# Rolling the columns of a matrix in HBM: DMA engines 516 rows apart in place of 4

## The chip, the cores and the metric

The kernel runs on one core of a Trainium2 chip. The metric is the device time of one execution in microseconds (us), the median of several runs. The work is nearly all DMA: 16 DMA engines of the core copy from HBM to HBM. Instructions on SP (SyncE), ACT (ScalarE) and POOL (GpSimd) issue the DMAs, each in its own queue; the 16 engines take the work of all queues.

## The reference

```
x = randn(8192, 8192) as float32, shift = 100
return np.roll(x, shift, axis=1)
```

Each row of 8192 numbers (32 KiB) is turned to the right by 100 places: columns 100 to 8191 of the output are columns 0 to 8091 of the input, and the last 100 columns of the input come first. Nothing is computed, and rows don't depend on each other.

## The kernel before

The output's columns are cut at `a` = 128, the shift rounded up to a multiple of 128; `g` = 28 is the rest. The columns from 128 on are the **main copy**: 8064 numbers, 32,256 bytes in each row, copied straight from `x` to `out`, both in HBM (L33 to L36). The first 128 columns, the **heads**, go through on-chip memory (L55 to L75): POOL loads small pieces into the tiles `t` and `h` (L66, L67, L70), VectorE puts the pieces together (L68, L71), and POOL stores them (L75). The heads are 8.39 MB of the DMA queues' 272.70 MB, and run beside the main copy in the first third of the time.

The main copy is one DMA for 16 rows. The 16 rows of a DMA are given to the 16 DMA engines, one to each. In the view `(c e j) w -> c j e w`, with 16 values of `e` and 4 of `j`, engine `e` gets row 64c + 4e + j: the engines stand 4 rows (128 KiB) apart within one block of 64 rows (2 MiB). The loop over `j` is the inner one, so that an engine takes four neighbouring rows one after the other; then `c` goes to the next block. DMAs with even `j` are issued by SP, with odd `j` by ACT: 256 each. No order between the DMAs is needed; each queue's issue waits for the DMA that it issued four places earlier, so that up to four DMAs of a queue are in flight.

The 18 DMAs of the heads are issued by POOL and wait only for each other and for VectorE's copies.

Of the kernel before, what the change touches and what calls it, by code (L numbers as in the profile page):

```python
# [1 line left out]

# [4 lines left out]


@with_exitstack
def kernel(  # L10
    ctx: ExitStack,
    tc: tile.TileContext,
    x: bass.AP,
    shift: int,
    out: bass.AP,
):
    nc = tc.nc
    n_rows, n_cols = x.shape
    s = shift % n_cols
    a = -(-s // 128) * 128  # L20
    g = a - s
    P = nc.NUM_PARTITIONS
    engines = [nc.sync, nc.scalar]
    n_chunks = 16
    rows = n_rows // n_chunks

    xm = x.rearrange("(c e j) w -> c j e w", e=16, j=4)
    om = out.rearrange("(c e j) w -> c j e w", e=16, j=4)
    if a < n_cols:  # L33
        for c in range(n_rows // 64):
            for j in range(4):
                engines[j % 2].dma_start(out=om[c, j, :, a:], in_=xm[c, j, :, g:n_cols - s])  # L36
    if a == 0:
        return


    if a > 512:
        for i in range(n_chunks):
            r = slice(i * rows, (i + 1) * rows)
            nc.gpsimd.dma_start(out=out[r, :s], in_=x[r, n_cols - s:])
            if g > 0:
                nc.gpsimd.dma_start(out=out[r, s:a], in_=x[r, :g])
        return

    Q, J = 4, 8
    n_st = n_rows // (P * Q * J)
    reads = ctx.enter_context(tc.tile_pool(name="reads", bufs=n_st))  # L55
    heads = ctx.enter_context(tc.tile_pool(name="heads", bufs=n_st))
    xt = x.rearrange("(k p j q) c -> k q p j c", q=Q, j=J, p=P)
    ot = out.rearrange("(k p j q) c -> k q p j c", q=Q, j=J, p=P)
    tiles = []
    for k in range(n_st):  # L60
        t = reads.tile([P, Q - 1, J, a], x.dtype)
        h = heads.tile([P, Q, J, a], x.dtype)
        for q in range(1, Q):
            lead = bass.AP(tensor=x.tensor, offset=(k * P * J * Q + q) * n_cols - s,
                           ap=[[J * Q * n_cols, P], [Q * n_cols, J], [1, a]])
            nc.gpsimd.dma_start(out=t[:, q - 1], in_=lead)  # L66
        nc.gpsimd.dma_start(out=h[:, Q - 1, :, :s], in_=xt[k, Q - 1, :, :, n_cols - s:])  # L67
        nc.vector.tensor_copy(h[:, :Q - 1, :, :s], t[:, :, :, :s])  # L68
        if g > 0:
            nc.gpsimd.dma_start(out=h[:, 0, :, s:], in_=xt[k, 0, :, :, :g])  # L70
            nc.vector.tensor_copy(h[:, 1:, :, s:], t[:, :, :, s:])  # L71
        tiles.append(h)
    for k, h in enumerate(tiles):
        for q in range(Q):
            nc.gpsimd.dma_start(out=ot[k, q, :, :, :a], in_=h[:, q])  # L75


# [1 line left out]
_INS = ['x', 'shift']  # L79
_OUTS = [((8192, 8192), 'float32')]  # L80

_NUMBERS = {'shift': 100}


# [26 lines left out]
```

## Time and profile before

| what | value |
|---|---|
| median of 7 runs | 821.04 us (818.74 to 822.83) |
| the profiled execution | 820.11 us, of which the span is 818.3 |
| instructions | 589; VectorE busy 3.7 us, POOL 16.1 us |
| issue of a main DMA on SP, on ACT | 0.51 us, 0.52 us (median) |
| main DMA from issue to landing | 12.5 us (median) |
| all DMAs that write `out`, from issue to landing | 4.1 us (least), 115.9 us (most) |

The span is the time from the first to the last instruction of the profiled execution. The page cuts it into 40 equal slices and gives, for each, the busy share of the DMA engines in tenths and the GB/s that they moved, counting each byte once. In the list of DMA queues, q1 is the queue of SP, q10 that of ACT and q0 that of POOL: the columns are packets, megabytes (MB), and the time that the packets took as a share of 16 engines over the stretch shown. A row of the main copy is one packet of 32,256 bytes and one of 4 bytes that reports its completion.

A line of waits gives who waited, at which line, for what: the sum in us, how often, and the longest. In the table of stretches, a line begins with the stretch, its length, the busy time of VectorE and POOL, and ends with the granted clock, the busy share of the DMA engines and the GB/s moved.

### The profile page before, as it was taken

To read this page: it belongs to the slowest core of one execution; us is meant where nothing else is said; L and a number is where in the kernel's file an instruction comes from. 1 tells how busy PE (TensorE), PEld (TensorE's weight loads), DVE (VectorE), ACT (ScalarE), POOL (GpSimd) and SP (SyncE) were. 2 spreads that over 40 slices of the span, in tenths; PEclk is the share of its full clock that TensorE was granted. 3 is DMA by queue.
4 is the path that set the end of the run, shared out by engine and by line. 5 is a ranking of instruction groups with operands and counts; after the bars stand their busy time and mean duration, and the time that the engine had idled before them with its cause. 6 is when DMAs were issued, how large, how long until landed. Compare 5 with 4: busy or idle time off the path is not lost. (4 is left out here: it accounts for less than half of the span.)

```text
span 818.3 us, 589 instructions
## 1 busy us (share of the span) xinstructions
DVE 3.7 (0%) x4; POOL 16.1 (2%) x22
## 2 busy tenths in 40 slices
DVE  0000000000000000000000000000000000000000
POOL 3001001000000000000000000000000000000000
DMA  9999999999999999999999999999999999999997
GB/s 301 335 341 334 330 344 361 356 351 351 342 352 335 326 328 334 341 326 336 334 330 328 339 328 334 337 331 331 334 326 337 337 325 333 330 333 337 328 337 255
DMA packets 18724, 272.70 MB, mean 333 GB/s; under 512 B 8480, under 2 KB 8480, under 8 KB 10528
## 3 DMA queue, kind: packets, MB, share of 16 engines
q1 hardware_dynamic: 8192, 132.14, 48.2%
q10 hardware_dynamic: 8192, 132.14, 46.3%
q0 software_dynamic: 2336, 8.39, 4.4%
q14 instruction: 4, 0.03, 0.0%
HBM read 268.44 MB, written 268.44 MB: 656 GB/s over the span
## 5 line engine op out<-in xcount | busy, mean ns | idle before, releaser
L75 POOL DMA_DIRECT2D out_dram<-h x8 | 6.9, 957 | 90.5 <-DMA h<-in_x_dram 79.5
L66 POOL DMA_DIRECT2D t<-in_x_dram x6 | 5.4, 912 | 0.8 <-PEq L106 0.8
L68 DVE COPY h<-t 128x2400 f32<-128x2400 f32 x2 | 2.8, 1410 | 115.8 <-DMA t<-in_x_dram 115.8
L67 POOL DMA_DIRECT2D h<-in_x_dram x2 | 1.8, 884 | 17.5 <-DMA t<-in_x_dram 17.5
L70 POOL DMA_DIRECT2D h<-in_x_dram x2 | 1.8, 884 | 13.1 <-DMA t<-in_x_dram 13.1
L71 DVE COPY h<-t 128x672 f32<-128x672 f32 x2 | 1.0, 505 | 0.0
L92 POOL MEMSET const-float32-0.0<- 128x1 f32 x1 | 0.1, 100 | 0.2 <-issue 0.2
L92 POOL MEMSET const-bfloat16-1.0<- 128x1 bf16 x1 | 0.1, 103 | 0.0
L92 POOL MEMSET const-float32-1.0<- 128x1 f32 x1 | 0.1, 100 | 0.0
L92 POOL MEMSET const-uint8-127<- 128x1 uint8 x1 | 0.1, 100 | 0.0
## 6 DMA issues: line engine op xcount, KB each, us to landing
out_dram<-in_x_dram ACTq DMA_DIRECT2D x256, 504.0 KB, 12.5
out_dram<-in_x_dram SPq DMA_DIRECT2D x256, 504.0 KB, 12.5
out_dram<-h POOLq DMA_DIRECT2D x8, 512.0 KB, 97.1
t<-in_x_dram POOLq DMA_DIRECT2D x6, 512.0 KB, 66.7
h<-in_x_dram POOLq DMA_DIRECT2D x2, 400.0 KB, 83.2
h<-in_x_dram POOLq DMA_DIRECT2D x2, 112.0 KB, 81.1
```

What stands on the lines that cost most here:

```text
L66: nc.gpsimd.dma_start(out=t[:, q - 1], in_=lead)
L67: nc.gpsimd.dma_start(out=h[:, Q - 1, :, :s], in_=xt[k, Q - 1, :, :, n_cols - s:])
L68: nc.vector.tensor_copy(h[:, :Q - 1, :, :s], t[:, :, :, :s])
L70: nc.gpsimd.dma_start(out=h[:, 0, :, s:], in_=xt[k, 0, :, :, :g])
L71: nc.vector.tensor_copy(h[:, 1:, :, s:], t[:, :, :, s:])
L75: nc.gpsimd.dma_start(out=ot[k, q, :, :, :a], in_=h[:, q])
L92: nc = _bacc.Bacc("TRN2", target_bir_lowering=False, num_devices=1)
```

## The change

The rows of the main copy are put into DMAs in another order. Engine `e` gets an area of its own that begins at row 516e (`pitch` = 8192/16 + 4). A DMA takes rows 516e + 4q + 64i + j for e = 0 to 15: neighbouring engines are 516 rows apart (16 MiB and 128 KiB). The innermost loop steps `j` by one row, the next `i` by 64 rows (7 steps), the outer one `q` by 4 rows (16 steps). This covers 448 rows of each area with 448 DMAs.

What is left is copied after q = 7, a little past the middle: 64 rows of each of the areas 0 to 14 in 60 DMAs of 16 rows that are 4 rows apart, as before; the 4 rows in each of these areas that follow in 4 DMAs of 15 rows; and the last 4 rows of the matrix in 4 DMAs of one row. There are 516 main DMAs in place of 512, 258 on each of SP and ACT. In the built kernel each of the one-row DMAs is 16 pieces of 504 numbers (2,016 bytes).

The heads, the columns of the main copy and the choice of queue by `j` are unchanged.

```diff
-    xm = x.rearrange("(c e j) w -> c j e w", e=16, j=4)
-    om = out.rearrange("(c e j) w -> c j e w", e=16, j=4)
+    pitch, steps = n_rows // 16 + 4, n_rows // 16 // 64 - 1
+    run = steps * 64
+
+    def main(n, first, step, count):
+        o = bass.AP(tensor=out.tensor, offset=first * n_cols + a, ap=[[step * n_cols, count], [1, n_cols - a]])
+        i = bass.AP(tensor=x.tensor, offset=first * n_cols + g, ap=[[step * n_cols, count], [1, n_cols - a]])
+        engines[n % 2].dma_start(out=o, in_=i)
+
     if a < n_cols:
-        for c in range(n_rows // 64):
-            for j in range(4):
-                engines[j % 2].dma_start(out=om[c, j, :, a:], in_=xm[c, j, :, g:n_cols - s])
+        for q in range(16):
+            for i in range(steps):
+                for j in range(4):
+                    main(j, 4 * q + 64 * i + j, pitch, 16)
+            if q == 7:
+                for e in range(15):
+                    for j in range(4):
+                        main(j, pitch * e + run + j, 4, 16)
+                for j in range(4):
+                    main(j, run + 64 + j, pitch, 15)
+                    main(j, n_rows - 4 + j, 1, 1)
```

## The prediction

> **What bounds the kernel now.** I read the page first, then the waits of SP's queue, then the DMA view cut to two stretches, then a table of stretches of 20 us.
>
> ```profile
> DMA  9999999999999999999999999999999999999997
> GB/s 301 335 341 334 330 344 361 356 351 351 342 352 335 326 328 334 341 326 336 334 330 328 339 328 334 337 331 331 334 326 337 337 325 333 330 333 337 328 337 255
> ...
> q1 hardware_dynamic: 8192, 132.14, 48.2%
> q10 hardware_dynamic: 8192, 132.14, 46.3%
> q0 software_dynamic: 2336, 8.39, 4.4%
> ...
> HBM read 268.44 MB, written 268.44 MB: 656 GB/s over the span
> ```
>
> The DMA engines are busy from the first slice to the last but one; VectorE and GpSimd together have 20 us of work. The two main queues, q1 (SP's) and q10 (ACT's), hold 94.5 of the 98.9% of engine time. Each has 8192 packets for 256 DMAs of 16 rows, two to a row: the row of 32,256 bytes and a completion of 4 bytes. One row is one engine's work. The waits of SP's queue say that the issue is not late:
>
> ```profile
> SPq L36 <- DMA out_dram<-in_x_dram: 670.8, 252, 5.2
> ```
>
> SP spent 670.8 of 818.3 us waiting for its own DMA four places back, so issue has slack. The end is therefore set by how long an engine takes for a row. The DMA view of 280 to 800 us, when only the main copy runs, and of 40 to 120 us, when the small "heads" run beside it, price a row:
>
> ```profile
> DMA packets 10722, 172.87 MB, mean 332 GB/s; under 512 B 5362, under 2 KB 5362, under 8 KB 5362
> ...
> q1 hardware_dynamic: 5361, 86.42, 51.5%
> q10 hardware_dynamic: 5359, 86.42, 48.0%
> ```
>
> ```profile
> q10 hardware_dynamic: 755, 12.23, 41.8%
> q1 hardware_dynamic: 752, 12.13, 38.7%
> q0 software_dynamic: 773, 2.77, 20.1%
> ```
>
> First stretch: 86.42 MB are 2679 rows of 32,260 bytes; 51.5% of 16 engines x 520 us is 4285 us, so 1.60 us a row on q1, and 1.49 us on q10, 1.545 us in the mean. Second stretch: 535 us for 379 rows, 1.41 us on q10, and 495 us for 376 rows, 1.32 us on q1, 1.36 us in the mean. The same row on the same engine takes 12% less time when a fifth of the engine time goes to something that moves little. So an engine's own speed is not what holds a row at 1.545 us; what it shares with the others does. Counting the main bytes twice (read and written in HBM) and the heads' once (their other end is on the chip), HBM carried 2 x 172.84 / 520 = 665 GB/s in the first stretch and (2 x 24.36 + 2.77) / 80 = 644 GB/s in the second. The rate of HBM under this pattern of addresses is the bound.
>
> **The change part by part.**
>
> *The order of rows.* 448 of the 512 former DMAs (87.5%) now have their 16 rows 516 apart in place of 4. The bytes, the row length, the two queues and the wait for the fourth DMA back are as before (the built kernel has the same waits on SP and ACT, and POOL's and VectorE's instructions in the same order). Each engine still takes four neighbouring rows and then goes 64 rows on. What is new is only that the engines stand in 16 separate areas, 16 MiB and 128 KiB apart, where they stood in one block of 2 MiB. Before has no stretch with such spacing, so I bound the cost by how much the rate moves in rows of before:
>
> ```profile
> 640.00:660.00 20.00, 0.00 (x0) 0.00 (x0) 1.00 1.01 342
> ...
> 680.00:700.00 20.00, 0.00 (x0) 0.00 (x0) 1.00 0.98 321
> ```
>
> The last column is GB/s. With the same work and the same spacing, stretches of 20 us go from 321 to 342 around 332. Nothing in the program differs between them, only how far the engines have drifted apart and so where they meet in memory. The ends:
> - Below: the best slice of 13 us in the view of 280 to 800 us has 345 GB/s. Held for all newly spaced rows this is 1 - 332/345 = 3.8% of 0.875 x 820.1 = 717.6 us, a gain of 27.0 us.
> - Above: the first 40 us, in which the heads' short pieces start up beside the main copy, have 316 GB/s. Held throughout, 332/316 - 1 = 5.1% of 717.6 us, a loss of 36.3 us.
>
> I take a point between the mean of 332 and the best 20 us of 342, that is 337 GB/s: 1 - 332/337 = 1.5%, a gain of 10.6 us. The reason is that the neighbours' positions in one 2 MiB block are the only thing that the program lets the 16 engines share, and the spread of the 20 us stretches says that this sharing costs something that comes and goes. I don't take 342, since no 80 us stretch before holds more than 335.
>
> *A rule that speaks against it.* The trace shows 128 KiB between engines going at 665 GB/s and no other spacing. The Trainium skill's page "DMA: Bandwidth & Descriptors", section "Latency and other measured facts", has copies in HBM that fall from 207 to 103 GB/s when the row pitch grows from 512 KiB to 4 MiB, and come back to 214 when 4 KiB are added to the pitch. By the rule without the pad the newly spaced rows would take about twice as long, an estimate of 1,540 us; by the rule with the pad, for which the 128 KiB beyond 16 MiB would count, nothing is lost. No run here shows either yet. The page "HBM Reference", section "Specifications (TRN2)", gives 716 GB/s for the memory that two cores share; the 536.9 MB that the page counts would need an estimate of 750 us by it, so it forbids a large gain and allows a small one.
>
> *The leftover rows.* Each engine's area is cut after 448 rows. After q = 7, 60 DMAs take 960 rows with the old spacing of 4: the same price as before, 1.545 us a row. Four DMAs take 15 rows each; engines 0 to 14 have 448 + 60 + 4 = 512 rows as before, the sixteenth 508, which gains nothing since the others end later. Four DMAs take one row each, which the built kernel splits into 16 pieces of 2,016 bytes. A sixteenth of a row is 0.10 us; a packet of the heads (2336 packets in 4.4% of 16 x 818.3 us, 3.6 KB in the mean) 0.25 us. So the four cost an engine between 0.4 and 1.0 us; I take 0.5 us. Two more issues per queue, of 0.51 us each, lie inside the 670.8 us of waiting. At this place two of the four DMAs that a queue may have in flight are small. The other two of each queue still give an engine four rows, 6.2 us of work, against 4.1 us for the quickest DMA from issue to landing: covered, so nothing. Without cover it would be 4.1 us, once.
>
> *The heads.* POOL's 18 DMAs and VectorE's four copies keep their places. They end at 262 us by the trace's packets, far ahead of the end. That main DMAs now run beside them in other places is in the bounds above.
>
> *The sum.* 820.1 (profiled: span 818.3 and 1.8 around it) - 10.6 + 0.5 = 810.0 us. The median of the runs is 0.9 us above the profiled execution, so 810.9, rounded to **811 us**.
>
> **The rivals.**
>
> *Slower: the far apart areas cost the memory more.* In the trace the one stretch in which HBM is asked for many scattered places at once, 40 to 120 us, carries 644 GB/s against 665. If sixteen separate areas to read and sixteen to write act like this, the newly spaced rows take 665/644 - 1 = 3.3% longer: 23.4 us, 844.9, or **845 us**. It decides from the first DMA on and lasts as long as the new spacing does; it wins as soon as what is lost by distance is above what is gained by engines not meeting, that is below 332 GB/s in the main stretch. For it: 665 GB/s is flat over 500 us (80 us stretches have 330 to 335), which looks like a memory that already works well, with little left to win. Against it: the rows in 40 to 120 us were quicker, not slower, and the heads' pieces of 512 bytes may be to blame for that rate in place of distance.
>
> *No difference: the change does nothing for the memory.* 516 is 8 x 64 + 4. Row 516e + 4q + 64i + j stands at place 4(e + q) + j in its block of 64 rows, and 4e + j was its place before: the engines differ by the same 4 rows within 2 MiB. If only the place inside 2 MiB matters, all stays at 332 GB/s, and the time is **821 us**, plus the 0.5 of the leftovers. For it: the flat rate. Against it: 321 to 342 GB/s in equal work.
>
> *A hole at the leftovers.* If the cover named above fails, 4.1 us are added to any of these; it changes no sign except near zero, and is in the ranges.
>
> **How the numbers follow.** I give the forecast (faster) 0.47, no difference 0.10, the slower rival 0.43. About 0.2% is what a measurement of this kernel can tell from no change. The likeliest case's own range is 794 (the gain of 27.0 us, less 0.5) to 819; the range over all cases runs to the upper end of the slower one, 821.0 + 36.3 + 0.5 = 858. I leave about 0.07 of the chance below 794, where HBM would have to carry more than any stretch shows, and 0.07 above 858.
>
> **What would show it.** In the DMA view of the changed kernel: the time of a row on q1 and q10 after the heads (1.545 us now) under 1.53 for the forecast, at it for no difference, near 1.60 for the slower rival; the slices' GB/s at 337, 332 or 322. The 60 leftover DMAs in the middle, about 95 us long, keep the old spacing: there the rate should fall back to 332, so that the slices before and after them show the change against itself. The wait of SP's queue should shrink with the span and not otherwise; a slice with DMA under 9 tenths beside the leftovers would be the hole. The prediction is wrong if the rate inside the leftovers equals that outside while the time has moved, for then the spacing is not the cause.

## The result and the profile after

The changed kernel takes **825.31 us** (median of 13 runs, 822.51 to 828.86) against 820.75 us (34 runs): a ratio of 1.0055, with a 95% interval of 1.0045 to 1.0065. The forecast was 811, with 0.43 on slower. The loss is 4.6 us where the forecast had a gain of 10.1. The times of single runs of one kernel lie within some 4 to 6 us, so that a profile, which is one run, can't show by itself where a loss of 2 us comes from.

The page of the changed kernel answers to the page lines shown in the prediction:

```profile
span 823.6 us, 593 instructions
...
DMA  9999999999999999999999999999999999999997
GB/s 299 340 335 338 338 346 354 350 350 344 349 335 334 332 327 324 331 332 337 331 326 329 321 326 327 331 329 331 329 327 331 328 342 331 332 321 335 327 331 263
...
q1 hardware_dynamic: 8252, 132.14, 48.0%
q10 hardware_dynamic: 8252, 132.14, 46.8%
q0 software_dynamic: 2336, 8.39, 4.3%
...
HBM read 268.44 MB, written 268.44 MB: 652 GB/s over the span
```

The bytes are the same, over the whole span the DMA engines are as full, and the heads' queue is as before. The rate is lower: 652 GB/s in HBM for 656. The 60 packets more on each main queue are the one-row DMAs in pieces (64 more), less two rows that the 15-row DMAs lack (4 fewer). SP's queue still waits most of the time, so issue is not late:

```profile
SPq L38 <- DMA out_dram<-in_x_dram: 672.6, 252, 3.7
```

The DMA view of 280 to 800 us, the stretch that the prediction used; its first line has the busy tenths in 40 slices of 13 us, which are all nines in the kernel before:

```profile
DMA  9999999999999989999999999999999999999999
DMA packets 10737, 171.28 MB, mean 329 GB/s; under 512 B 5366, under 2 KB 5430, under 8 KB 5430
...
q1 hardware_dynamic: 5369, 85.65, 50.7%
q10 hardware_dynamic: 5366, 85.62, 49.1%
```

By the same working as before, 85.65 MB are 2655 rows and 50.7% of 16 x 520 us is 4218 us: 1.59 us a row on q1, and 1.54 us on q10, 1.56 us in the mean for 1.545. Where in that stretch the rate is lost shows in two tables of the same four stretches. The last columns are the busy share of the DMA engines and GB/s. First the kernel before:

```profile
280.00:460.00 180.00, 0.00 (x0) 0.00 (x0) 1.00 0.99 332
460.00:490.00 30.00, 0.00 (x0) 0.00 (x0) 1.00 1.00 333
490.00:790.00 300.00, 0.00 (x0) 0.00 (x0) 1.00 1.00 333
```

Then the changed kernel, whose odd DMAs (15 rows, one row) are issued at 457 to 466 us and whose 64 small pieces run at 462 to 471 us:

```profile
280.00:460.00 180.00, 0.00 (x0) 0.00 (x0) 1.00 1.00 330
460.00:490.00 30.00, 0.00 (x0) 0.00 (x0) 1.00 0.94 316
490.00:790.00 300.00, 0.00 (x0) 0.00 (x0) 1.00 1.00 331
```

Around the odd DMAs the engines are idle for 6% of 30 us, and the rate falls to 316, below the 321 to 342 between which stretches of 20 us go in the kernel before: 30 x (1 - 316/331) = 1.4 us. It is the slice of 8 tenths above. Everywhere else the engines are as busy as before and move 0.6% less: 2/332 of 180 us and 2/333 of 300 us, 2.9 us. The first loss stands out of the swing; the second doesn't, since equal stretches of 100 us in the kernel before have 331 to 335.

The prediction had a test of its own: inside the 60 leftover DMAs with the old spacing the rate should go back. They are issued at 364 to 454 us, so 370 to 455 us shows them without the odd DMAs. First the changed kernel:

```profile
280.00:365.00 85.00, 0.00 (x0) 0.00 (x0) 1.00 1.00 330
370.00:455.00 85.00, 0.00 (x0) 0.00 (x0) 1.00 1.00 331
475.00:790.00 315.00, 0.00 (x0) 0.00 (x0) 1.00 1.00 330
```

Then the kernel before:

```profile
280.00:365.00 85.00, 0.00 (x0) 0.00 (x0) 1.00 0.99 332
370.00:455.00 85.00, 0.00 (x0) 0.00 (x0) 1.00 0.99 332
475.00:790.00 315.00, 0.00 (x0) 0.00 (x0) 1.00 0.99 332
```

Inside the leftovers the rate is 1 GB/s above what is around them and 1 below that of before. The prediction called itself wrong about the cause if the rates inside and outside were equal; a step of 1 GB/s is less than the swing, so this test decides nothing. What the spacing does by itself has to come from the medians of kernels that have it alone.

### The profile page after: what moved, and what is told of

Its sections match the earlier page's. It is cut to its first block, busy times and chain, and to the rows that moved or that the text cites. A ratio compares the mean times of both kernels' runs of the same rounds, so it can differ in the third digit from the quotient of the medians.

```text
span 823.6 us, 593 instructions
## 1 busy us (share of the span) xinstructions
DVE 3.7 (0%) x4; POOL 16.1 (2%) x22
```

## The experiments

Each is the main copy written anew with the change's helper `main(queue, first row, rows between engines, count)`; the heads stay as they are. Every kernel copies all rows. Ratios are to runs of the kernel before on the same chip, with 95% intervals; 0.1% is 0.8 us.

The theories at the outset: **D**, distance of the engines lowers the rate of HBM; **L**, the odd DMAs cost the time.

**One block in odd DMAs (e1_odd).**

```diff
     for c in range(n_rows // 64):
         for j in range(4):
+            if c == 72:
+                main(j, 64 * c + j, 4, 15)
+                main(j, 64 * c + 60 + j, 1, 1)
+            else:
                 main(j, 64 * c + j, 4, 16)
```

> The old spacing of 4 rows throughout; only one block of 64 rows, past the middle, is copied by four DMAs of 15 rows and four of one row, as the change's last leftovers are. If distance is the cause of the 4.6 us (theory D), this is at 821.0 to 821.6 us. If the odd DMAs are the cause (theory L), 824 to 826 us.

822.35 us, ratio 1.0027 (1.0014 to 1.0039). Between the two: the odd DMAs cost something, but not all. In the same stretches this kernel has less of a hole than the changed kernel, 30 x (1 - 326/332) = 0.5 us, which is within the swing of the kernel before. Its last stretch has 331, as in the changed kernel, though its spacing is the old one, so that the 331 there can't be laid to the 516 rows:

```profile
280.00:460.00 180.00, 0.00 (x0) 0.00 (x0) 1.00 1.00 333
460.00:490.00 30.00, 0.00 (x0) 0.00 (x0) 1.00 0.97 326
490.00:790.00 300.00, 0.00 (x0) 0.00 (x0) 1.00 1.00 331
```

**508 rows apart, whole DMAs (e2_p508).**

```diff
+    for q in range(16):
+        for i in range(8):
+            if 4 * q + 64 * i < 508:
+                for j in range(4):
+                    main(j, 4 * q + 64 * i + j, 508, 16)
+        if q == 7:
+            for j in range(4):
+                main(j, 16 * 508 + j, 4, 16)
```

> Engines 508 rows apart (16 MiB less 128 KiB), stepping by 1, 64 and then 4 rows: the change's distance, with 512 whole DMAs of 16 rows and no odd ones; only the last 64 rows keep the old spacing, past the middle. Theory D: 825 to 826 us, and 329 to 331 GB/s after the heads. Theory L: 820 to 822 us.

821.69 us, ratio 1.0011 (0.9997 to 1.0026). With nearly the change's distance, no loss that can be told from none (the interval ends at 2.1 us). D in its simple form falls.

**512 rows apart (e3_p512).**

```diff
+    for q in range(16):
+        for i in range(8):
+            for j in range(4):
+                main(j, 4 * q + 64 * i + j, 512, 16)
```

> Engines exactly 512 rows (16 MiB) apart, stepping by 1, 64 and then 4 rows, 512 whole DMAs. All engines then stand at the same place of their block of 64 rows. If the place within 2 MiB is what counts for HBM, this is much slower: 900 us or more. If only distance counts (D): 825 us. Theory L: 821 us.

2347.98 us, the median of six runs that lie far apart (2021.75 to 2420.12): 2.5 to 2.9 times as long. From its page, which shows the run of 2021.75:

```profile
GB/s 129 134 131 127 135 136 148 146 139 139 147 151 138 142 144 141 128 135 128 131 132 128 135 131 135 141 145 146 139 134 130 129 128 135 130 126 130 129 130 117
...
q10 hardware_dynamic: 8192, 132.14, 52.8%
q1 hardware_dynamic: 8192, 132.14, 44.6%
...
HBM read 268.44 MB, written 268.44 MB: 266 GB/s over the span
```

The engines are busy throughout and a row takes (52.8% + 44.6%) x 16 x 2020 us / 8192 = 3.8 us. Apart from the last 64 rows, the work, the DMAs and the order of steps differ from the run at 508 by four rows of spacing alone. So rows 512 apart are in each other's way, and four rows less put it right.

**68 rows apart (e4_p68).**

```diff
+    for b in range(7):
+        for q in range(17):
+            for j in range(4):
+                main(j, 1088 * b + 4 * q + j, 68, 16)
+    for c in range(9):
+        for j in range(4):
+            main(j, 7616 + 64 * c + j, 4, 16)
```

> Engines 68 rows (2 MiB and 128 KiB) apart in seven areas of 1088 rows, stepping by 1 and 4 rows, 448 + 28 DMAs with this spacing and the last 36 with the old one. Theory D with a price that grows with the distance: 821.5 to 824 us; with a price for leaving the 2 MiB block at all: 825 us. Theory L: 821 us.

832.72 us, ratio 1.0146 (1.0128 to 1.0165). A nearer spacing costs ten times what 508 rows cost: no theory had this. I formed another, **M**: an engine's place in the pattern of 64 rows moves at each step of q to the place that its neighbour has just left, and each move costs. Here there are 112 moves, in the run at 508 about 15.

**Old spacing with moves (e5_rot), 68 rows with few moves (e6_p68keep), 508 rows with many (e7_p508walk).** The cores of the three:

```diff
+    for b in range(7):                                    # e5_rot
+        for c in range(16):
+            for j in range(4):
+                main(j, 1088 * b + 68 * c + j, 4, 16)
+        for j in range(4):
+            main(j, 1088 * b + 64 + j, 68, 16)
...
-    for b in range(7):                                    # e6_p68keep, against e4_p68
-        for q in range(17):
+    for q in range(17):
+        for b in range(7):
...
+    for q in range(127):                                  # e7_p508walk
+        for j in range(4):
+            main(j, 4 * q + j, 508, 16)
```

> The old spacing of 4 rows in one 64-row stretch, but each stretch begins 68 rows after the one before, so that every engine's place in the 64-row pattern moves on by 4 rows (to where its neighbour was) after every four DMAs: 112 such moves, and no far distance. Theory M (each move of place costs about 0.11 us, from the 12.2 us of the run with 68 rows over its 112 moves): 832 to 834 us. Theory D (distance of the engines costs): 820.5 to 822 us.

> Engines 68 rows apart as in the run at 832.7 us, the same DMAs in another order: by 1, 1088 and then 4 rows, so that an engine keeps its place in the 64-row pattern for seven groups of four and moves 16 times in all. Theory M: 821.5 to 823 us. Theory D: 832 us.

> Engines 508 rows apart as in the run at 821.7 us, the same DMAs in another order: by 1 and then 4 rows through each engine's area, so that the place moves after every four DMAs, 126 times. Theory M: 833 to 836 us. Theory D: 821.7 us.

823.49 us, ratio 1.0036 (1.0022 to 1.0050); 839.58 us, ratio 1.0236 (1.0214 to 1.0259); 823.82 us, ratio 1.0047 (1.0032 to 1.0061). None of the three came out as M or D had it. M falls as the cause of the 12 us: with a seventh of the moves, 68 rows are slower still. But a small price goes along with moves: 0.36% or 3.0 us for 112 moves of the old spacing, and 0.47 - 0.11 = 0.36% (0.16 to 0.57, an estimate from the two intervals) for 111 moves more at 508 rows, 0.027 us a move in place of 0.11. Neither pair changes the moves alone. Against what was expected of it, e5_rot does have a far spacing in the four DMAs at the end of each `b`: 28 DMAs are 68 rows apart, an estimate of 0.7 to 1.1 us by the losses of e4_p68 and e6_p68keep over their 476 DMAs, which leaves 0.016 to 0.020 us a move. e7_p508walk walks through neighbouring rows where e2_p508 steps by 64. What is slow at 68 rows is the spacing. The view of 280 to 800 us of e6_p68keep has the loss in the rate, with the engines full:

```profile
DMA packets 10380, 167.38 MB, mean 322 GB/s; under 512 B 5190, under 2 KB 5190, under 8 KB 5190
...
q10 hardware_dynamic: 5188, 83.65, 50.1%
q1 hardware_dynamic: 5190, 83.71, 50.0%
```

**Five odd blocks (e8_odd5).** As e1_odd, with `c in (56, 72, 88, 104, 120)`.

> As the run with one block in DMAs of 15 rows and one row, with five such blocks (56, 72, 88, 104 and 120). If the 1.9 us of that run are the price of one such block, 828 to 832 us; if they were chance, 821 to 824 us.

822.76 us, ratio 1.0037 (1.0024 to 1.0050). This is in the range for chance, but clear of no change: five blocks cost 3.0 us, 0.6 us each (0.4 to 0.8), so that the 1.9 us of e1_odd can't be a fixed price of one.

**The change without odd DMAs (e9_whole516), 508 rows with them (e10_p508odd).**

```diff
             if q == 7:
+                for j in range(4):
+                    main(j, 448 + j, 516, 16)
                 for e in range(15):
                     for j in range(4):
-                        main(j, pitch * e + run + j, 4, 16)
-                for j in range(4):
-                    main(j, run + 64 + j, pitch, 15)
-                    main(j, n_rows - 4 + j, 1, 1)
+                        main(j, 516 * e + 452 + j, 4, 16)
...
             for j in range(4):                            # e10_p508odd, against e2_p508
-                main(j, 16 * 508 + j, 4, 16)
+                main(j, 8128 + j, 4, 15)
+                main(j, 8188 + j, 1, 1)
```

> The change with its 516 rows and its order, but the leftovers in whole DMAs only: four DMAs of 16 rows 516 apart (rows 448 to 451 of each area and the last four rows of the matrix) and 60 of 16 rows 4 apart. 512 main DMAs, none of 15 rows or of one. If the odd DMAs are a part of the 4.6 us as in the run that has them alone (1.9 us), 822.3 to 823.7 us; if the spacing of 516 rows is all of it, 824.5 to 825.5 us; if all comes from the odd DMAs, 820.5 to 821.5 us.

> 508 rows apart as in the run at 821.7 us, with its last 64 rows, past the middle, in four DMAs of 15 rows and four of one row. If the odd DMAs cost as much beside far spacing as in the old one, 822.7 to 824 us; if they cost little, 821.5 to 822.3 us; if the combination costs more than its parts, 824.5 us or more.

822.83 us, ratio 1.0029 (1.0019 to 1.0040); 823.67 us, ratio 1.0039 (1.0024 to 1.0053). Taking the odd DMAs out of the change gives back 0.26% (0.11 to 0.41); putting them into the run at 508 rows adds 0.28% (0.07 to 0.49). Both intervals are estimates from those of the two ratios. Both times are where a part for the odd DMAs had been expected. In these stretches of e9_whole516 the hole is gone, and the rate elsewhere is between that of before and that of the change:

```profile
280.00:460.00 180.00, 0.00 (x0) 0.00 (x0) 1.00 1.00 331
460.00:490.00 30.00, 0.00 (x0) 0.00 (x0) 1.00 1.00 333
490.00:790.00 300.00, 0.00 (x0) 0.00 (x0) 1.00 1.00 332
```

**511 rows and one row apart (e11_p511, e12_p1).**

```diff
+    for q in range(16):                                   # e11_p511
+        for i in range(8):
+            for j in range(4):
+                if 4 * q + 64 * i + j < 511:
+                    main(j, 4 * q + 64 * i + j, 511, 16)
+        if q == 7:
+            main(3, 16 * 511, 1, 16)
...
+    for c in range(n_rows // 64):                         # e12_p1
+        for j in range(4):
+            main(j, 64 * c + 16 * j, 1, 16)
```

> Engines 511 rows apart, 16 MiB less one row of 32 KiB, in place of 508, stepping by 1, 64 and then 4 rows. At 512 rows the time was 2348 us, at 508 it was 821.7 us. If any offset of a whole row is enough for HBM, 821 to 824 us; if the 16 engines have to stand on places that differ by the four rows that each works through, 850 us or more.

> Engines one row apart: each DMA is 16 neighbouring rows, and four of them make a block of 64 rows. No far distance, all offsets of 32 KiB. If any offset of a whole row is enough, 818 to 824 us; if 4 rows are needed, 850 us or more.

856.41 us, ratio 1.0443 (1.0418 to 1.0469); 828.89 us, ratio 1.0098 (1.0068 to 1.0128). One row (32 KiB) less than 512 undoes most of the loss (2348 to 856 us), four rows nearly all of it (822 us). One row apart with no distance costs 1.0%, far less than 856 us would have it. The two are no clean pair: at 511 rows an engine takes four neighbouring rows, in e12_p1 its rows are 16 apart.

**Where the odd DMAs' price comes from.** Four kernels with the old spacing: the odd block early (f1_oddearly, block 4) or late (f2_oddlate, block 120); its one-row DMAs spread over the four blocks that follow (f3_oddspread); four DMAs of 7560 columns and four of 504 in their place, with all 16 engines at work (f4_small).

```diff
-            if c == 72:                                   # f1_oddearly, f2_oddlate
+            if c == 4:                                    # 120 in f2_oddlate
...
             if c == 72:                                   # f3_oddspread
                 main(j, 64 * c + j, 4, 15)
-                main(j, 64 * c + 60 + j, 1, 1)
...
+        if 73 <= c <= 76:
+            main(c - 73, 64 * 72 + 60 + c - 73, 1, 1)
...
+                part(j, 64 * c + j, 0, 7560)              # f4_small, part: main of these columns
+                part(j, 64 * c + j, 7560, n_cols - a)
```

> The old spacing, with block 4 of 128 in DMAs of 15 rows and of one row (before: 72). If the price is paid at the place (theory P), 821.9 to 822.7 us as with block 72. If the engines run worse from then on because one is ahead (theory A), more than with block 72, 823.5 us or more.

> The old spacing, with block 120 of 128 in odd DMAs. Theory P: 821.9 to 822.7 us. Theory A: 820.3 to 820.8 us, since only 6% of the rows follow.

> The old spacing, block 72 in four DMAs of 15 rows, and its four one-row DMAs one after each of the next four blocks, so that a queue always has at least three whole DMAs in flight. If the hole is the price, 820.3 to 821.0 us; if theory A, 822.0 to 822.7 us.

> The old spacing, block 72 in four DMAs of 16 rows by 7560 numbers and four of 16 rows by 504 numbers, in the places that the odd ones had: small DMAs and as few bytes in flight, but every engine has the same work and its own rows. If the hole is the price, 822 to 822.7 us; if theory A or the shared rows are, 820.3 to 821.0 us.

821.43 us, ratio 1.0015 (1.0003 to 1.0027); 820.79 us, 0.9998 (0.9985 to 1.0011); 820.92 us, 1.0006 (0.9997 to 1.0014); 821.65 us, 1.0015 (1.0005 to 1.0025). Theory A falls: early costs no more than at block 72, and f4_small, in which no engine is ahead, costs 0.15% as well; only block 120 came out as A had it. Theory P does not hold either, since blocks 4 and 120 are below its range. f3_oddspread came out as the hole had it, f4_small just below. Small DMAs among few others cost 1.2 us (0.4 to 2.1) even with equal work; where they are spread the cost is not to be told from none, nor from that of f1_oddearly, whose interval overlaps. The stretch of 30 us around the odd DMAs, for f4_small, f2_oddlate, f1_oddearly and f3_oddspread:

```profile
460.00:490.00 30.00, 0.00 (x0) 0.00 (x0) 1.00 0.95 318
...
755.00:785.00 30.00, 0.00 (x0) 0.00 (x0) 1.00 0.91 322
...
24.00:54.00 30.00, 1.83 (x2) 1.76 (x2) 1.00 1.00 344
...
460.00:490.00 30.00, 0.00 (x0) 0.00 (x0) 1.00 0.97 337
```

So the hole is there in f4_small and not when the small DMAs are spread. But it is also there at block 120, where the time does not change, and not at block 4, beside the heads, where it does by 0.15%. At block 120 the end makes up for it in the one trace: from 785 us on the engines are busy for 0.90 of the time, against 0.84 in the kernel before:

```profile
785.00:819.00 34.00, 0.00 (x0) 0.00 (x0) 1.00 0.90 299
...
785.00:818.30 33.30, 0.00 (x0) 0.00 (x0) 1.00 0.84 290
```

That the hole is the price of the odd DMAs is thus likely for the middle of the kernel, and not shown.

**8 and 20 rows apart (g1_p8, g2_p20).**

```diff
+    for c in range(n_rows // 128):                        # g1_p8
+        for j in range(8):
+            main(j, 128 * c + j, 8, 16)
...
+    for q in range(5):                                    # g2_p20
+        for b in range(25):
+            for j in range(4):
+                main(j, 320 * b + 4 * q + j, 20, 16)
+        if q == 2:
+            for c in range(3):
+                for j in range(4):
+                    main(j, 8000 + 64 * c + j, 4, 16)
```

> Engines 8 rows apart, each taking 8 neighbouring rows, blocks of 128 rows, 512 whole DMAs. Engines e and e + 8 then stand on the same place of two neighbouring blocks of 64 rows. If the places within 64 rows have to differ (as the run at 512 rows suggests), 850 us or more; if the pattern of HBM is longer than 64 rows, 818 to 823 us.

> Engines 20 rows apart in areas of 320 rows, stepping by 1, 320 and then 4 rows: 16 different places within 64 rows, each kept for 25 groups of four, and 640 KiB between neighbours. If only the places count, 820 to 821.5 us; if leaving the 64-row block costs, 822.5 us or more.

827.48 us, ratio 1.0075 (1.0052 to 1.0097); 833.53 us, ratio 1.0156 (1.0136 to 1.0176). With 8 rows two engines at a time share a place within 64 rows, and it costs 0.75%, not the many per cent expected: 64 rows are not to HBM what 512 are. (Each engine also takes eight neighbouring rows here, not four.) With 20 rows all 16 places differ, and it costs twice as much: the place within 64 rows is not the whole rule.

## Why the prediction was wrong

- **The bound.** That the addresses can set the end is shown by e3_p512: the same DMAs with other addresses run 2.5 to 2.9 times as long, with the engines full. That HBM, and not the engines, holds the spacing of 4 rows at 332 GB/s is supported, not proven. The DMA queues of the kernel before at 120 to 160 us and at 160 to 240 us:

```profile
q10 hardware_dynamic: 387, 6.19, 44.0%
q1 hardware_dynamic: 391, 6.32, 42.4%
q0 software_dynamic: 473, 1.69, 14.0%
...
q10 hardware_dynamic: 783, 12.71, 46.3%
q1 hardware_dynamic: 778, 12.55, 45.8%
q0 software_dynamic: 695, 2.49, 8.0%
```

With the main bytes counted twice and the heads' once, HBM carried 668 and 663 GB/s there, against 665 from 280 us on, while what the engines moved fell from 355 over 347 to 332. The 644 of 40 to 120 us fit less well.
- **The step that failed is the choice of 337 GB/s for the newly spaced rows.** I took the swing of 321 to 342 GB/s between stretches of 20 us as the price of meeting in one block of 2 MiB, which 16 areas would remove. The changed kernel swings as widely (slices of 321 to 342 after the heads), and its mean is 329, not 337: 2 x 171.27 / 520 = 659 GB/s in HBM for 665; outside the hole it is 330 to 331. The term was -10.6 us. In e9_whole516, where only the order of steps stands beside it, it is +2.4 us (1.6 to 3.3): the spacing brings no gain. Where the swing comes from stays open.
- **The rival "no difference" came nearest, and I gave it 0.10.** It said that 516 rows keep the 4 rows between engines within the 2 MiB block. The runs fit a form of it: whole multiples of 512 rows do nothing to keep engines out of each other's way (512 rows: 2348 us), so that 516 is to HBM nearly what 4 is, and 508 what 4 is in the other direction (821.7 us). The period of 64 rows in that rival was wrong, as 8 and 20 rows show. The 512 is argued from 508, 511, 512 and 516, not measured for its own sake, and 511 (856 us) beside one row (829 us) fits in sign only.
- **The slower rival had the sign, not the cause.** Distance as such has no price of 3.3%: 508 rows have +0.1%, while 20 and 68 rows have 1.5 to 2.4%. The time of a row, 1.56 us, is also nearer to no difference than to the 1.60 of this rival.
- **The leftovers were 0.5 us; with the odd DMAs taken out of the change, the time falls by about 2 us** (0.9 to 3.3; one such block by itself 0.0 to 0.27%, five of them 0.37%). Their packets were no dearer than predicted: nearly all of the 64 pieces of 2,016 bytes took 0.08 us each. What failed is the cover, 6.2 us of rows in flight against 4.1 us for the quickest landing: the one-row DMAs themselves took 7.0 us to land (median), and the engines are 6% idle around them. The cover also left out that DMAs of 15 rows give the sixteenth engine no row. The rival "a hole at the leftovers" had the sign that it named, a slice under 9 tenths, and 4.1 us; the idle time and the lost rate come to 1.4 us.
- **The order of steps was taken as nothing.** Each step of q moves an engine to its neighbour's former place. The change has 15 such moves in the main loop and some 15 among the 60 leftovers: 0.5 to 0.8 us, an estimate from the two pairs above, in which other things changed too.
- **Two readings were off, without weight in the sum.** The heads' last packets are at 252 us, not 262, and "no 80 us stretch before holds more than 335" is true from 240 us on: beside the heads, 160 to 240 us holds 347.
- **The Trainium skill's rule.** The page "DMA: Bandwidth & Descriptors", section "Latency and other measured facts", has copies whose rate halves at a row pitch of 4 MiB, a large power of two, and is restored by 4 KiB on top. The runs agree in kind: 512 rows (16 MiB) move 135 GB/s by the profile of the quickest run, 508 rows 331 after the heads. They differ in size: 32 KiB less than 16 MiB (511 rows) still cost 4.4% here, 128 KiB less (508) nothing that can be told, and 128 KiB more (516 in whole DMAs) 0.3%.

**The account** of the 4.6 us: about 2 us for the odd DMAs (0.9 to 3.3), of which the trace shows 1.4 as a hole, and 2.4 us (1.6 to 3.3) for the rows 516 apart in the order of the change. Of the 2.4 us, the moves may be 0.5 to 0.8; the rest is open. It can't be told from what 508 rows cost, whose interval ends at 2.1 us, and the one trace of e9_whole516 doesn't place it in the main stretch: from 280 to 800 us it moved 172.74 MB for 172.87, which is 0.4 of the 2.1 us by which that run is longer than the profiled one of before.

## What to carry to other kernels

When engines stream side by side, don't go by how far apart they are, and try spacings a few rows off a large power of two: here 512 rows between engines took 2.5 to 2.9 times as long and 508 rows no time that can be told. Swings of a rate between equal stretches are no proof that a part of the loss can be removed, and a difference that a test is to read in a trace has to be larger than they are. Odd DMAs that make a tiling come out even should be reshaped into whole ones where that is possible, which gave back about 2 us here; their bytes alone are not their price.

## What the runs showed of the hardware

- Spacing of the 16 engines against time: 4 rows 820.5 us, 508 rows 821.7, 516 in whole DMAs 822.8, 8 rows 827.5, one row 828.9, 68 rows 832.7 and 839.6, 20 rows 833.5, 511 rows 856.4, 512 rows 2348 (2022 to 2420). No order by distance runs through this list. It is not spacing alone at 8 rows and at one row, where an engine's own steps differ too.
- At 68 rows the same DMAs in two orders differ by 6.9 us (ratios 1.0146 and 1.0236); the order in which an engine keeps its place in the 64-row pattern for seven groups of four DMAs is the slower one.
- No spacing tried beat 4 rows in one block of 64: HBM moved 665 GB/s there, reads and writes together, over 520 us.
- Around four 15-row and four one-row DMAs in the middle of the change the 16 engines were busy for 0.94 of 30 us; at 508 rows, with the same odd DMAs, for 0.95.
